# Two ordinary weight tiles after each Strassen tile, and SwiGLU outputs of that stage kept in fp32 until it ends

## The chip, the core and the metric

The kernel runs on one core of a Trainium2 chip. The metric is the device time in microseconds of one execution, taken as the median of the runs. A separate execution is taken with the hardware profiler, and all rows of a trace come from that one. Five engines work side by side, each with a queue of its own: TensorE (PE in the profile, with PEld for its weight loads), VectorE (DVE), ScalarE (ACT), GpSimd (POOL) and SyncE (SP, which issues nearly all DMAs here).

## What is computed

A decoder trunk of two layers on 256 tokens of width 2048, all in float32. The first layer is a recurrent block (RG-LRU) and a SwiGLU feed-forward, the second a sliding-window attention and a SwiGLU feed-forward. The change touches the feed-forward alone, which runs once in each layer:

```python
D_MODEL = 2048; SEQ = 256; D_FF = 5632
def swiglu_ffn(x, g, w_in, w_out):      # w_in: 2048 x 11264, w_out: 5632 x 2048
    h = rms_norm(x, g)
    gate, up = jnp.split(h @ w_in, 2, axis=-1)
    return x + (jax.nn.silu(gate) * up) @ w_out
```

## The kernel before

**Tiles and precision.** Every weight matrix is read once from HBM, as tiles of 128 x 1024 floats (512 KB): 256 rows of the matrix by 512 columns, that is two row blocks of 128 and four column blocks of 128. A float32 product is made from fp32r parts: a number v is split into `hi`, its rounded copy, and `lo = v - hi`, and the product is `hi*hi + hi*lo + lo*hi`, three matmuls of 128 x 256. So each weight tile costs ACT one copy (`hi<-raw`, line 295) and DVE one subtraction (`lo<-raw,hi`, line 298), and then PE 2 x 4 x 3 = 24 matmuls (`products`, line 361). Activations are kept in the same two parts, in one slot of 128 x 512 that holds `hi` and `lo` of 128 features for 256 tokens. Slots (`s` in the profile) come from a first-in first-out list of 58.

**The stream.** All tiles stand in one list, `jobs`, and `stream` walks through it. At tile i it emits the DMA of tile i+4 (`load`), the split of tile i+3 (`split`) and the matmuls of tile i. There are four buffers each of `raw`, `hi` and `lo`, so the split of a tile needs the `hi` buffer of the tile four before it, and a DMA needs the split of the tile four before. Work that is not tied to a tile (epilogues, norms, the attention) is written as generators; `run_bg` steps them twice per tile as long as two running estimates, `self.dve` and `self.act`, stay under a budget. A generator that yields n sleeps n half tiles.

**Ordinary and Strassen tiles.** The 11264 columns of `ffn_in` make 22 groups of 512 columns, 8 tiles each (the 2048 rows). A group holds gate, up, gate, up for two blocks of 128 hidden features. Groups 4 to 21 are *ordinary* (`group`). Groups 0 to 3 (`NS = 4`) are *Strassen* groups: a tile is taken as a 2 x 2 block product and made with 7 block products instead of 8, so 21 matmuls instead of 24 (`strassen`, line 460). For this the tile needs sums of its blocks: `sums` puts three subtractions on POOL (lines 277 to 279, `s<-raw`), and `split` then has three pairs to split instead of one (line 287 on ACT, line 288 on DVE: one 128 x 768 piece `lo<-raw,hi` and two 128 x 512 pieces `s<-s,s`). It also needs sums of the activation blocks, made once for each feed-forward by `form` (lines 488 to 491 on POOL, then a split).

**The order of tiles.** `ffn` writes it by hand: 4 ordinary tiles (`AHEAD`), then Strassen and ordinary tiles in turn, 32 of each, then the remaining ordinary tiles. This stretch, from the first to the last Strassen tile, is called the Strassen stage below; there is one in each feed-forward. A Strassen group holds 4 PSUM banks of the 8 for all its tiles. The ordinary groups beside it are `paired`: their four results share two banks. Unpaired groups take four banks and make some products as one matmul of 128 x 512 instead of two of 128 x 256 (the `"h"` parts in `products`).

**Epilogues.** When a Strassen group ends, `fast` takes its 4 banks to two slots U and V (DVE and ACT), applies SiLU, multiplies gate and up with `stt` (line 134), and four PE transposes (lines 369 and 372) bring the result to features by tokens; then two splits make `hid`, the parts that `ffn_out` will need. When an ordinary group ends, `done` pulls four results, applies SiLU, multiplies (`tt`, line 130) and splits twice. `hid` is first read by `project`, which runs after all of `ffn_in`.

Of the kernel before, what the change touches and what calls it, by code (L numbers as in the profile page):

```python
# [12 lines left out]
F32 = mybir.dt.float32  # L13
F32R = mybir.dt.float32r
AF = mybir.ActivationFunctionType
ALU = mybir.AluOpType
# [3 lines left out]
T = 256  # L20
DFF = 5632
ND = D // P
# [27 lines left out]
class Trunk:  # L50
# [17 lines left out]

    NS = 4
    AHEAD = 4  # L70
    SPACE = 14

    def __init__(self, ctx, tc, dram):
# [355 lines left out]
                    done([(p, two, st["bank"][b] if last_of else None) for p, two, b, last_of in st["ps"]])  # L429
            jobs.append((src(c), mm))  # L430

    def strassen(self, src, xs, forms, done, last):

        st = {}
        jobs = []
        for c in range(ND // 2):
            part = {}

            def mm(hi, lo, c=c, part=part):
                if c == 0:  # L440
                    st["ps"] = [self.bank() for _ in range(4)]
                    st["begun"] = set()
                ps = st["ps"]
                x2 = [self.need(xs[2 * c + kt]) for kt in range(2)]
                fh, fl = self.need(forms[c])
                A = lambda kt, b: tuple(x2[kt][:, q + b * P:q + b * P + P] for q in (0, T))
                S = lambda n: tuple(q[:, n * P:n * P + P] for q in (fh, fl))
                B = lambda n: tuple(q[:, n * T:n * T + T] for q in (hi, lo))
                s = part["set"]
                t1, t3, t2, t4 = (tuple(s[n + q][:, h * T:h * T + T] for q in (0, 1)) for n in (2, 4) for h in range(2))  # L450
                todo = [(0, 0, A(0, 0), B(1)), (1, 1, A(1, 0), B(3)), (1, 0, S(1), t2), (2, 0, S(0), t1),
                        (2, 1, S(2), t3), (3, 0, S(3), B(2)), (3, 1, A(1, 1), t4)]
                if self.other is not None:
                    self.runs = self.RUNS
                    self.other = None
                for n, (b, h, w, m) in enumerate(todo):
                    if n == 4:
                        self.half_tick()
                    for i, j in ((0, 0), (0, 1), (1, 0)):
                        self.nc.tensor.matmul(ps[b][:, h * T:h * T + T], w[i], m[j], start=b not in st["begun"],  # L460
                                              stop=c == ND // 2 - 1 and i == 1, skip_group_check=True)
                        st["begun"].add(b)
                        self.since += 1
                if last and c == ND // 2 - 1:
                    for q in self.sets:
                        for t in q:
                            self.free(t)
                    self.sets = None
                if last:
                    for q in (fh, fl):  # L470
                        self.free(q)
                if c == ND // 2 - 1:
                    done(ps)
            jobs.append((src(c), mm, part))
        return jobs

    def form(self, c, col, out):

        while len(self.slots) < self.SPACE:
            yield 1  # L480
# [156 lines left out]
    def ffn(self, l, xs, forms, r, gains, rn, out=None):  # L637
        hid = [Val() for _ in range(NH)]
        w = self.d[f"ffn_in{l}"]
        one = self.con[:, K_ID:K_ID + P]  # L640
        turns, ordinary = [], []
        for g in range(self.NS):
            def fast(ps, g=g):
                c1, U, V = self.t(), self.slot(F32), self.slot(F32)
                two = lambda q: q.rearrange("p (b t) -> p b t", b=2)
                twice = lambda q: q.unsqueeze(1).broadcast_to([P, 2, T])
                self.a(c1, ps[0][:, 0:T])
                self.tt(two(U[:, :]), two(ps[1][:, :]), twice(c1[:, :]), ALU.add)
                self.tt(two(V[:, :]), two(ps[2][:, :]), twice(U[:, 0:T]), ALU.add)
                self.tt(U[:, 0:T], ps[2][:, 0:T], V[:, T:2 * T], ALU.add)  # L650
                self.tt(V, ps[3], V, ALU.add)
                for b in ps:
                    self.free_bank(b)

                def task():
                    while not self.rv[r].ready:
                        yield 1
                    rs = [self.rstd[r][:, T + b:T + b + 1] for b in range(2)]
                    for q, s in ((U, 0), (V, 1)):
                        self.a(q[:, T:2 * T], q[:, T:2 * T], AF.Silu, scale=rs[s])  # L660
                    yield
                    for q, k, s in ((V, U, 0), (U, V, 1)):
                        self.stt(q[:, 0:T], q[:, 0:T], rs[s], k[:, T:2 * T], ALU.mult, ALU.mult)
                    yield 4
                    while not self.room():
                        yield 1
                    p = self.mbank()
                    for h in range(2):
                        for b, q in enumerate((V, U)):
                            self.pe_other(p[:, h * T + b * P:h * T + b * P + P], q[:, h * P:h * P + P], one,  # L670
                                          f=self.nc.tensor.transpose)
                    yield 1
                    self.free(U)
                    self.free(V)
                    for h in range(2):
                        while not self.slots:
                            yield 1
                        s = self.slot()
                        self.split_act(s, p[:, h * T:h * T + T])
                        hid[2 * g + h].ap = s  # L680
                        hid[2 * g + h].ready = True
                        yield
                    self.free_mbank(p)
                self.spawn(task())
            turns += self.strassen(lambda c, g=g: w[g, c], xs, forms, fast, g == self.NS - 1)
        for g in range(self.NS, NH // 2):
            def done(ps, g=g):
                rs = self.rstd[r][:, 0:T]
                early = not self.rv[r].ready
                v = [self.pull(p, r=None if early else rs) for p in ps]  # L690

                def task():
                    while not self.rv[r].ready:
                        yield 1
                    for h in range(2):
                        ga, up = v[2 * h], v[2 * h + 1]
                        if early:
                            self.tt(ga, ga, rs, ALU.mult)
                            self.tt(up, up, rs, ALU.mult)
                        self.a(ga, ga, AF.Silu)  # L700
                        yield
                        self.tt(ga, ga, up, ALU.mult)
                        while not self.slots:
                            yield 1
                        s = self.slot()
                        self.split_act(s, ga)
                        self.free_half(ga)
                        self.free_half(up)
                        hid[2 * g + h].ap = s
                        hid[2 * g + h].ready = True  # L710
                        yield
                self.spawn(task())
            self.group(lambda c, g=g: w[g, c], ND, xs, done, g == NH // 2 - 1, self.SYNC,
                       paired=2 * (g <= 2 * self.NS), jobs=ordinary)
        n = len(turns)
        self.jobs += ordinary[:self.AHEAD]
        for q in zip(turns, ordinary[self.AHEAD:]):
            self.jobs += q
        self.jobs += ordinary[self.AHEAD + n:]
        self.project(self.d[f"ffn_out{l}"], NH, hid, gains, rn, out)  # L720


# [610 lines left out]
```

## Time and profile before

| | us |
|---|---|
| median of 3 runs (range) | 2023.13 (2022.03 to 2024.72) |
| the profiled execution, its own time | 2023.72 |
| span of that execution, first to last instruction | 2021.9 |
| PE busy | 1985.0 (98%) |
| DVE busy | 1412.9 (70%) |
| ACT busy | 1122.3 (56%) |
| POOL busy | 376.7 (19%) |

A row of instruction groups reads: line, engine, operation, output<-input, shapes, count | busy us, mean ns of one | idle time of the engine before them and what ended it. A row of waits reads: engine, output and line that waited <- what it waited for: us in total, times, longest. A row of the timeline reads: start us, us, engine, line, operation, count. A row of windows gives for a stretch the busy time of PE, PEld, DVE, ACT and POOL (each with its count), the clock granted to PE, and the DMA share. A matmul of 128 x 256 is shown as some 276 ns long, but the next one starts after 113 to 118 ns; so a busy PE may still be late by up to 160 ns per matmul without a gap, and the starts are what to read. A few per cent of the matmul records are missing.

### The profile page before, as it was taken

The page shows a single profiled execution, that of the slowest core. Times are in us where ns is not written, and L with a number is a line of the kernel's source. Part 1 is how long each engine was busy: PE and PEld are TensorE (multiplying, and loading weights), DVE is VectorE, ACT ScalarE, POOL GpSimd, SP SyncE. Part 2 cuts the span into 40 slices and gives each one's busy share as a digit, 9 for nine tenths or more (in the row PEclk, how much of TensorE's full clock was granted, in tenths as well). Part 3 has the DMA queues.
Part 4 walks back from the last instruction along what each step waited for, and adds up shares of the span by engine and source line. Part 5 has one row for each costly group of instructions (what it writes and reads, how often), then busy time and mean ns, then how long its engine had stood idle before and what let it go on. Part 6 is the DMA issues. An engine that isn't in the chain of part 4 may idle for free.

```text
span 2021.9 us, 41009 instructions
## 1 busy us (share of the span) xinstructions
PE 1985.0 (98%) x16699; PEld 1943.6 (96%) x16699; DVE 1412.9 (70%) x2089; ACT 1122.3 (56%) x1754; POOL 376.7 (19%) x356
## 2 busy tenths in 40 slices
PE   9999998999999999999999999989999999999999
PEld 9999998999999999999999889889999999999999
DVE  8988979999655655545667767889866556554553
ACT  6799766555444444434556776555555445444342
POOL 0000136774000000000002453576700000000000
PEclk9999999999999999999999999999999999999999
DMA  8555654555555555555555435455555655556663
GB/s 279 189 182 186 209 173 161 188 180 193 194 198 191 196 192 195 193 194 198 190 190 164 139 123 175 160 173 182 176 192 192 196 195 190 197 197 201 207 209 125
DMA packets 106204, 377.15 MB, mean 187 GB/s; under 512 B 11936, under 2 KB 14368, under 8 KB 106016
## 3 DMA queue, kind: packets, MB, share of 16 engines
q1 hardware_dynamic: 105408, 373.88, 56.0%
q8 instruction: 130, 2.13, 0.4%
q10 hardware_dynamic: 608, 0.66, 0.1%
q14 instruction: 58, 0.48, 0.1%
HBM read 371.88 MB, written 2.10 MB: 185 GB/s over the span
## 4 chain that ended last, share of the span: by engine, by line
PE 83%; DVE 7%; issue 3%; ACT 3%; POOL 2%; DMA 1%; ACTq 0%; DVEq 0%; POOLq 0%; SPq 0%
PE b L361 75%; PE b L460 4%; DVE lo L298 2%; DVE s L288 2%; PE b L372 1%; DVE s L130 1%; ACT hi L295 1%; ACT s L121 1%; DMA raw<-in_ffn_in 1%; DVE lo L288 1%; PE b L826 1%; POOL s L277 1%; PE b L369 1%; POOL s L489 1%; PE b L1012 1%
## 5 line engine op out<-in xcount | busy, mean ns | idle before, releaser
L361 PE MATMUL b<-s,hi 128*128 128x256 f32 (+1 forms) x9474 | 1309.1, 284 | 6.1 <-ACT hi L295 4.9
L361 PEld LDWEIGHTS b<-s,hi 128*128 128x128 f32 x9474 | 1207.5, 189 | 29.0 <-ACT hi L295 5.3
L298 DVE TENSOR_TENSOR lo<-raw,hi 128x1024 fp32r<-128x1024 f32 (+1 forms) x643 | 795.7, 1240 | 501.8 <-ACT hi L295 497.8
L295 ACT ACTIVATE hi<-raw 128x1024 fp32r<-128x1024 f32 (+1 forms) x643 | 675.8, 1054 | 623.4 <-PE b L361 562.1
L361 PE MATMUL b<-s,lo 128*128 128x256 f32 x4992 | 753.1, 277 | 0.0
L361 PEld LDWEIGHTS b<-s,lo 128*128 128x128 f32 x4992 | 655.1, 189 | 0.6
L277 POOL TENSOR_TENSOR s<-raw 128x512 f32<-128x512 f32 x64 | 121.4, 1896 | 115.0 <-DMA raw<-in_ffn_in 98.1
L288 DVE TENSOR_TENSOR s<-s,s 128x512 fp32r<-128x512 f32 x128 | 125.8, 985 | 17.5 <-ACT s L287 17.5
L1102 POOL TENSOR_TENSOR s<-s 128x128 f32<-128x128 f32 x32 | 14.7, 461 | 635.3 <-ACT s L121 630.7
L287 ACT ACTIVATE s<-s 128x512 fp32r<-128x512 f32 x128 | 79.7, 624 | 87.0 <-POOL s L277 48.1
L460 PE MATMUL b<-s,s 128*128 128x256 f32 x768 | 115.4, 283 | 4.4 <-DVE s L288 4.2
L460 PEld LDWEIGHTS b<-s,s 128*128 128x128 f32 x768 | 100.9, 189 | 6.3 <-DVE s L288 6.2
L460 PE MATMUL b<-hi,s 128*128 128x256 f32 x384 | 89.4, 282 | 1.1 <-DVE s L130 0.9
L288 DVE TENSOR_TENSOR lo<-raw,hi 128x768 fp32r<-128x768 f32 x64 | 80.4, 1256 | 0.4
L279 POOL TENSOR_TENSOR s<-raw,s 128x256 f32<-128x256 f32 x64 | 72.5, 1132 | 5.0
L489 POOL TENSOR_TENSOR s<-s 128x128 f32<-128x128 f32 x16 | 16.3, 1017 | 303.4 <-ACT s L121 303.4
L121 ACT ACTIVATE s<-s 128x256 f32<-128x256 f32 (+3 forms) x132 | 51.9, 439 | 37.4 <-POOL s L491 26.4
L460 PEld LDWEIGHTS b<-hi,s 128*128 128x128 f32 x384 | 68.4, 190 | 1.9 <-DVE s L130 1.9
L278 POOL TENSOR_TENSOR s<-raw,s 128x256 f32<-128x256 f32 x64 | 66.5, 1040 | 5.0
L460 PE MATMUL b<-lo,s 128*128 128x256 f32 x192 | 54.6, 284 | 7.6 <-DVE lo L288 7.6
L121 ACT ACTIVATE s<-x,par 128x256 fp32r<-128x256 f32 (+1 forms) x112 | 52.7, 497 | 16.4 <-DVE x L130 11.2
L130 DVE TENSOR_TENSOR s<-s,s 128x256 fp32r<-128x256 f32 (+3 forms) x100 | 46.1, 489 | 20.9 <-ACT s L121 20.9
(120 smaller groups left out, 1188.6 us busy)
## 6 DMA issues: line engine op xcount, KB each, us to landing
raw<-in_ffn_in SPq DMA_DIRECT2D x352, 512.0 KB, 3.4
raw<-in_ffn_out SPq DMA_DIRECT2D x176, 512.0 KB, 3.3
raw<-in_lru_in SPq DMA_DIRECT2D x62, 512.0 KB, 3.6
raw<-in_lru_out SPq DMA_DIRECT2D x32, 512.0 KB, 4.2
raw<-in_w_q SPq DMA_DIRECT2D x32, 512.0 KB, 3.4
raw<-in_w_o SPq DMA_DIRECT2D x32, 512.0 KB, 3.3
raw<-in_gate SPq DMA_DIRECT2D x8, 512.0 KB, 3.7
raw<-in_kv SPq DMA_DIRECT2D x8, 512.0 KB, 4.3
```

The lines of the kernel that those rows point to most:

```text
L121: self.nc.scalar.activation(out, in_, func, **kw)
L130: self.nc.vector.tensor_tensor(out, a, b, op)
L277: tt(two(s[0][:, :]), b[:, 0:3:2, :], b[:, 1::-1, :], ALU.subtract)
L278: tt(s[1][:, 0:T], raw[:, 2 * T:3 * T], s[0][:, 0:T], ALU.subtract)
L279: tt(s[1][:, T:2 * T], raw[:, 3 * T:4 * T], s[1][:, 0:T], ALU.subtract)
L287: self.nc.scalar.activation(a, z, AF.Copy)
L288: self.nc.vector.tensor_tensor(b, z, a.bitcast(F32), ALU.subtract)
L295: high = self.ins(self.nc.scalar.activation(hi[:, q], raw[:, q], AF.Copy))
L298: self.nc.vector.tensor_tensor(lo[:, q], raw[:, q], hi[:, q].bitcast(F32), ALU.subtract)
L361: self.nc.tensor.matmul(*args, **kw)
L460: self.nc.tensor.matmul(ps[b][:, h * T:h * T + T], w[i], m[j], start=b not in st["begun"], stop=c == ND // 2 - 1 and i == 1, skip_group_ch ...
L489: tt(s[2], a11, a21, ALU.subtract)
```

## The change

After each Strassen tile come two ordinary tiles instead of one (`OWN = 2`), so that the 32 Strassen tiles of a feed-forward stand among 64 ordinary ones, and ordinary groups up to 12, not 8, are paired. Groups that end while Strassen tiles are still to come no longer split their SwiGLU outputs at once: the two blocks of a group are kept as one fp32 slot, and a new generator `later` splits them when the last Strassen tile has been emitted (`left[0]` is 0). A Strassen group copies its transposed result from PSUM with one ACT copy of 128 x 512 and splits from there.

```diff
-    def strassen(self, src, xs, forms, done, last):
+    def strassen(self, src, xs, forms, done, last, left):
 ...
+                left[0] -= 1
 ...
+        left = [self.NS * ND // 2]
+
+        def later(g, s):
+            while left[0]:
+                yield 1
+            for h in range(2):
+                while len(self.slots) < 2:
+                    yield 1
+                q = self.slot()
+                self.split_act(q, s[:, h * T:h * T + T])
+                hid[2 * g + h].ap = q
+                hid[2 * g + h].ready = True
+                yield
+            self.free(s)
 ...                                                  (fast, after the transposes into p)
-                    for h in range(2):
-                        while not self.slots:
-                            yield 1
-                        s = self.slot()
-                        self.split_act(s, p[:, h * T:h * T + T])
-                        hid[2 * g + h].ap = s
-                        hid[2 * g + h].ready = True
-                        yield
+                    s = self.slot(F32)
+                    self.a(s, p)
                     self.free_mbank(p)
+                    yield
+                    yield from later(g, s)
 ...                                                  (done of an ordinary group)
+                        if both is not None or h == 0 and left[0]:
+                            if h == 0:
+                                both = self.slot(F32)
+                            self.tt(both[:, h * T:h * T + T], ga, up, ALU.mult)
+                            self.free_half(ga)
+                            self.free_half(up)
+                            yield
+                            continue
 ...
+                    if both is not None:
+                        yield from later(g, both)
 ...
-                       paired=2 * (g <= 2 * self.NS), jobs=ordinary)
+                       paired=2 * (g <= (self.OWN + 1) * self.NS), jobs=ordinary)
 ...
-        for q in zip(turns, ordinary[self.AHEAD:]):
-            self.jobs += q
-        self.jobs += ordinary[self.AHEAD + n:]
+        for i, q in enumerate(turns):
+            k = self.AHEAD + self.OWN * i
+            self.jobs += [q] + ordinary[k:k + self.OWN]
+        self.jobs += ordinary[self.AHEAD + self.OWN * n:]
```

Counted over the whole built program, 63 matmuls of 128 x 512 become 126 of 128 x 256, and nothing else changes on PE but the order. SP issues the same 734 DMAs and POOL the same 361 instructions. DVE has 16 instructions fewer and ACT 8 fewer (results of unpaired groups come in two halves that are added; four groups in each feed-forward no longer need this). Twelve groups in each feed-forward, 4 Strassen and 8 ordinary, have their 24 splits put off. The line numbers of the changed kernel are one or more higher than those of the kernel before.

**DVE at the end of the first Strassen group.** Here `lo<-raw,hi` and `s<-s,s` are splits of coming tiles, `s<-b,...` take the four banks to U and V, and SCALAR_TENSOR_TENSOR are the two products that the transposes need. Before:

```order
L130 TENSOR_TENSOR s_4349<-b_85,t_92 128x512
L130 TENSOR_TENSOR s_4350<-b_86,s_4349 128x512
L288 TENSOR_TENSOR s_3724<-s_3721,s_3723 128x512
L130 TENSOR_TENSOR s_4349<-b_86,s_4350 128x256
L288 TENSOR_TENSOR lo_81<-raw_73,hi_77 128x768
L130 TENSOR_TENSOR s_4350<-b_87,s_4350 128x512
L288 TENSOR_TENSOR s_3726<-s_3722,s_3725 128x512
L298 TENSOR_TENSOR lo_82<-raw_74,hi_78 128x1024
L134 SCALAR_TENSOR_TENSOR s_4350<-s_4350,rstd_104,s_4349 128x256
L134 SCALAR_TENSOR_TENSOR s_4349<-s_4349,rstd_104,s_4350 128x256
```

Four splits of weight tiles stand among the four bank reads and ahead of the products. The same place in the changed kernel:

```order
L131 TENSOR_TENSOR s_4539<-b_85,t_92 128x512
L131 TENSOR_TENSOR s_4540<-b_86,s_4539 128x512
L131 TENSOR_TENSOR s_4539<-b_86,s_4540 128x256
L131 TENSOR_TENSOR s_4540<-b_87,s_4540 128x512
L299 TENSOR_TENSOR lo_80<-raw_72,hi_76 128x1024
L135 SCALAR_TENSOR_TENSOR s_4540<-s_4540,rstd_104,s_4539 128x256
L135 SCALAR_TENSOR_TENSOR s_4539<-s_4539,rstd_104,s_4540 128x256
```

Now one split stands ahead of the products. On PE, the four transposes of each of the first three groups stood 36 matmuls behind the last one of their group in the first feed-forward and 45 in the second; now they stand 69 and 60 behind it.

**POOL at the opening of the first Strassen stage.** L277 to L279 (L278 to L280 in the changed kernel) are the sums of one Strassen tile, the other rows are the last two `form`s. Before:

```order
L489 TENSOR_TENSOR s_3887<-s_3886 128x128
L488 TENSOR_TENSOR s_3887<-s_3886 128x128
L490 TENSOR_TENSOR s_3887<-s_3887,s_3886 128x128
L489 TENSOR_TENSOR s_3895<-s_3894 128x128
L491 TENSOR_TENSOR s_3887<-s_3886,s_3887 128x128
L277 TENSOR_TENSOR s_3715<-raw_71 128x512
L278 TENSOR_TENSOR s_3716<-raw_71,s_3715 128x256
L279 TENSOR_TENSOR s_3716<-raw_71,s_3716 128x256
L488 TENSOR_TENSOR s_3895<-s_3894 128x128
L490 TENSOR_TENSOR s_3895<-s_3895,s_3894 128x128
L491 TENSOR_TENSOR s_3895<-s_3894,s_3895 128x128
```

The third Strassen tile's sums stood inside the last form. The same place in the changed kernel:

```order
L491 TENSOR_TENSOR s_3853<-s_3852 128x128
L278 TENSOR_TENSOR s_3721<-raw_74 128x512
L490 TENSOR_TENSOR s_3853<-s_3852 128x128
L279 TENSOR_TENSOR s_3722<-raw_74,s_3721 128x256
L492 TENSOR_TENSOR s_3853<-s_3853,s_3852 128x128
L280 TENSOR_TENSOR s_3722<-raw_74,s_3722 128x256
L493 TENSOR_TENSOR s_3853<-s_3852,s_3853 128x128
L490 TENSOR_TENSOR s_3861<-s_3860 128x128
L491 TENSOR_TENSOR s_3861<-s_3860 128x128
L492 TENSOR_TENSOR s_3861<-s_3861,s_3860 128x128
L493 TENSOR_TENSOR s_3861<-s_3860,s_3861 128x128
```

The second Strassen tile's sums now stand among the steps of the form before the last, and the last form follows without a break.

More of the change, by code (lines that the diff above doesn't have):

```diff
@@ L70 @@
     AHEAD = 4
+    OWN = 2
     SPACE = 14
@@ L674, in task @@
                     self.free(V)
-                    for h in range(2):
-                        while not self.slots:
-                            yield 1
-                        s = self.slot()
-                        self.split_act(s, p[:, h * T:h * T + T])
-                        hid[2 * g + h].ap = s
-                        hid[2 * g + h].ready = True
-                        yield
+                    s = self.slot(F32)
+                    self.a(s, p)
                     self.free_mbank(p)
+                    yield
+                    yield from later(g, s)
                 self.spawn(task())
-            turns += self.strassen(lambda c, g=g: w[g, c], xs, forms, fast, g == self.NS - 1)
+            turns += self.strassen(lambda c, g=g: w[g, c], xs, forms, fast, g == self.NS - 1, left)
         for g in range(self.NS, NH // 2):
@@ L694, in task @@
                         yield 1
+                    both = None
                     for h in range(2):
```

## The prediction

> **What bounds the kernel now.** I read the page first, then the windows of the two Strassen stages beside a stretch of ordinary tiles, then PE's waits in each stage, and last the timeline for the length of single tiles.
>
> ```profile
> span 2021.9 us, 41009 instructions
> PE 1985.0 (98%) x16699; PEld 1943.6 (96%) x16699; DVE 1412.9 (70%) x2089; ACT 1122.3 (56%) x1754; POOL 376.7 (19%) x356
> PE   9999998999999999999999999989999999999999
> ```
>
> PE bounds the kernel nearly everywhere, so the time falls only where PE waits or runs slowly. The windows go from the first to the last Strassen matmul of each feed-forward; the third one holds ordinary tiles alone.
>
> ```profile
> 304.10:493.80 189.70, 175.18 (x1435) 171.01 (x1434) 176.78 (x195) 106.49 (x167) 130.29 (x98) 0.99 0.53 177
> 1287.00:1481.10 194.10, 178.91 (x1436) 176.05 (x1435) 175.73 (x197) 108.29 (x167) 131.70 (x98) 0.96 0.54 176
> 550.00:800.00 250.00, 250.00 (x2101) 245.69 (x2100) 151.72 (x212) 121.25 (x164) 0.00 (x0) 1.00 0.59 194
> ```
>
> In the stages PE is idle for 14.5 and 15.2 us, DVE is busy for 93% and 91%, POOL for 69% and 68%, and the granted clock dips. With ordinary tiles PE is never idle and DVE is at 61%. What PE waits for in the first stage, and then in the second:
>
> ```profile
> PE b L460 <- DVE lo L288: 5.5, 5, 1.6
> PE b L361 <- ACT hi L295: 4.7, 1, 4.7
> PE b L369 <- DVE s L134: 2.0, 3, 0.7
> PE b L460 <- DVE s L288: 1.4, 4, 0.8
> ```
> ```profile
> PE b L369 <- DVE s L134: 9.5, 3, 3.8
> PE b L460 <- DVE s L288: 2.9, 4, 1.9
> PE b L460 <- DVE lo L288: 2.0, 2, 1.8
> ```
>
> All but one are DVE being late: with the splits of a Strassen tile (L288) or with the products ahead of the transposes (L134). These idle times leave out what the modelled matmul ends cover, so I go by starts of tiles. An ordinary tile ahead of the stage, a Strassen and an ordinary tile inside it, and the ordinary tiles behind it, in the timeline of PE:
>
> ```profile
> 296.02 1.98 PE L361 MATMUL b<-s,hi 128*128 128x256 f32 x16
> ...
> 298.74 1.98 PE L361 MATMUL b<-s,hi 128*128 128x256 f32 x16
> ...
> 398.60 0.28 PE L460 MATMUL b<-hi,s 128*128 128x256 f32 x1
> ...
> 401.06 2.05 PE L361 MATMUL b<-s,hi 128*128 128x256 f32 x16
> ...
> 403.89 0.28 PE L460 MATMUL b<-hi,s 128*128 128x256 f32 x1
> ...
> 494.07 2.05 PE L361 MATMUL b<-s,hi 128*128 128x256 f32 x16
> ...
> 496.90 2.05 PE L361 MATMUL b<-s,hi 128*128 128x256 f32 x16
> ...
> 510.06 1.09 PE L361 MATMUL b<-s,hi 128*128 128x512 f32 x5
> ```
> ```profile
> L295 ACT ACTIVATE hi<-raw 128x1024 fp32r<-128x1024 f32 x92 | 97.7, 1062 | 128.1 <-PE b L361 110.1 <-issue 18.0
> ```
>
> An ordinary tile takes 2.72 us outside the stage (296.02 to 298.74; 92 tiles in the window of 250 us give 2.72 too). Inside it takes 2.83 us even where nothing waits (401.06 to 403.89), and so still behind it (494.07 to 496.90), until unpaired groups with 128x512 matmuls begin at 510. A Strassen tile without a wait takes 2.46 us. So without any wait a stage would be 32 x 2.46 + 31 x 2.83 + about 2 for 18 small matmuls (transposes, norm) = 168.4 us. It takes 189.7 and 194.1: **21.3 and 25.7 us are lost**, 47 in all.
>
> **The change part by part.**
>
> *More ordinary tiles in the stage.* 31 tiles for each feed-forward move from behind the stage, where they cost 2.72 us, between its first and last Strassen tile, where they cost 2.83. A stage without waits is then 32 x 2.46 + 62 x 2.83 + 2 = 256.2 us; today's stage with the 31 tiles behind it is 189.7 + 84.3 = 274.0 and 194.1 + 84.3 = 278.4. The most that the change can bring is so 17.8 + 22.2 = 40 us. It holds the price of the slower pace, 2 x 31 x 0.11 = 6.8 us, already. That price is bounded by 0 (the paired tiles at 296 ran at 2.72 with no Strassen tile among them) and 6.8; I take 6.8, since the paired tiles at 494 to 500 kept the pace of the stage with no Strassen tile left.
>
> *What is left of the waits* depends on DVE's share. The rows of DVE that grow, go or wait, first stage, then the split of an ordinary tile and of an output outside it:
>
> ```profile
> L298 DVE TENSOR_TENSOR lo<-raw,hi 128x1024 fp32r<-128x1024 f32 x33 | 46.9, 1424 | 0.3
> L130 DVE TENSOR_TENSOR s<-h,s 128x256 fp32r<-128x256 f32 x8 | 7.2, 897 | 0.0
> L130 DVE TENSOR_TENSOR s<-b,s 128x256 fp32r<-128x256 f32 x6 | 2.5, 417 | 0.0
> L288 DVE TENSOR_TENSOR s<-s,s 128x512 fp32r<-128x512 f32 x63 | 63.9, 1016 | 6.4 <-ACT s L287 6.4
> ```
> ```profile
> L298 DVE TENSOR_TENSOR lo<-raw,hi 128x1024 fp32r<-128x1024 f32 x92 | 112.6, 1224 | 98.8 <-ACT hi L295 98.6
> L130 DVE TENSOR_TENSOR s<-h,s 128x256 fp32r<-128x256 f32 x24 | 9.0, 419 | 0.0
> L121 ACT ACTIVATE s<-h 128x256 fp32r<-128x256 f32 x24 | 8.5, 402 | 0.0
> ```
>
> DVE's 176.8 us in the first stage gain 31 splits of 1.42 = 44, and four ordinary epilogues of six instructions of about 0.42 = 10; the output splits, 7.2 for the ordinary groups and 2.5 for the Strassen ones, leave. That makes 221 us in 256, 86% instead of 93%. POOL's 130 us spread to 51%. A split may be about two tiles late before PE notices (it is emitted three tiles ahead), and the slack of a Strassen tile with its two neighbours is 8.12 - 221 / 32 = 1.2 us, where today the work of a pair, 176.8 / 32 = 5.5, stands against 5.29 of PE. So DVE turns from late to early, and PE is the bound. What I leave of the waits, each between 0 and what it is today:
>
> - Splits of Strassen tiles (L288): 6.9 and 4.9 us today. Left: 1 in each stage.
> - Transposes (L369 behind L134): 2.0 and 9.5 us. The order shown in the section on the change has one split instead of four ahead of the products, and 69 and 60 matmuls instead of 36 and 45 to cover them, 8.1 and 7.1 us at 2.83 / 24 = 0.118. Today's worst case shows the queue of DVE:
>
> ```profile
> 1344.34 0.68 DVE L130 TENSOR_TENSOR s<-b,s 128x512 f32<-128x512 f32 x1
> ...
> 1345.54 0.87 DVE L134 SCALAR_TENSOR_TENSOR s<-s,rstd,s 128x256 f32<-128x256 f32 x2
> ...
> 1346.07 0.47 PE L369 MATMUL b<-con,s 128*128 128x128 f32 x1 [3.83 <-DVE s L134]
> ```
> ```profile
> 1346.00:1352.00 6.00, 5.93 (x29) 5.72 (x30) 3.95 (x7) 2.85 (x6) 4.14 (x3) 0.54 0.62 208
> ```
>
>   There 45 matmuls (5.3 us) were 3.83 us too few, so 9.1 would have been needed with DVE four splits behind; in the first stage 36 matmuls (4.2) were 0.7 too few, so 4.9. Both are the ends; three splits fewer (each 0.7 to 1.2) bring the worst to about 6, under 7.1. Left: 0.5 and 1.5. With the wait goes the half clock behind it: 6 us at 0.54 cost 2.8.
> - The opening: in the first stage 4.7 us (PE waits for a `hi` of ACT, which is blocked behind a form that POOL has not finished, the row below), in the second the L288 waits of 1.9 and 1.8. The last form no longer has sums in its middle, but the norm (its reciprocal and products) and the forms still fall on DVE and POOL there. Left: 2.5 and 2.5.
>
> ```profile
> 315.15 0.63 ACT L121 ACTIVATE s<-s 128x512 fp32r<-128x512 f32 x1 [4.20 <-POOL s L491]
> ```
>
> - The put-off splits: 24 x 0.42 us on DVE and 24 x 0.40 on ACT, 10 us of each behind each stage, where DVE is busy for 61% and ACT for 48%, so some 25 us of slack lie in each 65 us of tiles; `project` reads `hid` hundreds of us later. They cost between 0 and 10 a feed-forward; I take 0.5. The whole 128x512 ACT copies and the fp32 slots lie beside matmuls: ACT has 44% of the stage free, and PE's ordinary tiles do not read them.
>
> The sum left is 2 + 2 + 5 + 1 = 10 us, so 40 - 10 = 30 us gained. The profiled execution took 2023.72 us, of which 1.8 lie outside the span; 2023.7 - 30 = 1993.7. The median is 0.6 below that execution, so **1993 us**.
>
> **The rivals.**
>
> *DVE and POOL exclude each other, and half of the loss stays.* DVE's splits and POOL's sums both read slots, and both get longer together. Their shortest durations beside their medians in the first stage:
>
> ```profile
> L288 DVE TENSOR_TENSOR s<-s,s x63: 676/691/1792, 303.9 to 489.4; 128x512 fp32r<-128x512 f32 x63
> L288 DVE TENSOR_TENSOR lo<-raw,hi x31: 943/1104/2052, 307.9 to 488.5; 128x768 fp32r<-128x768 f32 x31
> L298 DVE TENSOR_TENSOR lo<-raw,hi x33: 1209/1217/2315, 304.9 to 491.1; 128x1024 fp32r<-128x1024 f32 x33
> L277 POOL TENSOR_TENSOR s<-raw x30: 1267/1740/4153, 310.2 to 482.0; 128x512 f32<-128x512 f32 x30
> L278 POOL TENSOR_TENSOR s<-raw,s x30: 737/1068/1806, 311.8 to 483.5; 128x256 f32<-128x256 f32 x30
> L279 POOL TENSOR_TENSOR s<-raw,s x30: 723/1097/1603, 312.9 to 484.7; 128x256 f32<-128x256 f32 x30
> ```
>
> The shortest times add up to 42.6 + 29.2 + 39.9 on DVE and 81.8 on POOL, 193.5 us, and about 11 us of epilogue products come on top: 204 in a stage of 189.7. So they overlap a little, and nearly exclude each other. Taken as one resource they would need 204 + 31 x 1.21 = 242 of the new 256 us, 95%, which leaves bursts (openings, group ends) hardly any room. If half of today's 47 us stayed, the time would be 2023.7 - 40 + 23.5 = 2007. Against it stands that 204 is already 8% more than the stage took; scaled so, 242 is 225, 88%. The Trainium skill, "SBUF — State Buffer", section "Who interferes with whom", says that a DVE instruction with two SBUF inputs and a GpSimd instruction that reads SBUF block each other for the whole instruction; by that rule the sum would be this rival's 2007, by DVE's own busy share it is 1993. The trace agrees with it only in part, by the 204 in 189.7. Chance 0.16.
>
> *Slower: the loss belongs to each Strassen tile, not to DVE's share.* If a Strassen tile's own chain (DMA, sums on POOL, copies on ACT, splits on DVE) is what is late, each of the 64 tiles keeps its 47 / 64 = 0.73 us, and the slower pace of 6.8 us is all that is added: 2030. It decides from 40 us left, 0.63 a tile. For it: PE's waits are at L460 and L369, Strassen work. Against it: the chain has one ordinary tile more of room, and DVE itself waits only 6.4 us on ACT in the first stage. Chance 0.06.
>
> *The put-off splits are exposed.* If all 10 us of them fell on PE in each feed-forward, 1993.7 + 20 = 2013. DVE's 39% of free time there speaks against it. Chance 0.03.
>
> *The pace of 2.72 comes back inside the stage.* 124 ordinary tiles x 0.11 = 13.6 us more: 1980. Nothing but the tiles at 296 speaks for it. Chance 0.03.
>
> **How the numbers follow.** The forecast itself, 5 to 22 us left of the waits, has 0.72: 1988 to 2005. A measurement of this kernel can tell about 0.2%, 4 us, from no change. Faster by more: the forecast, most of the first rival and the last two, 0.90; within: the far end of the first rival, 0.04; slower: 0.06. The low end, 1984, is the sum with no wait left (40 us), the high end, 2011, takes in most of the first rival.
>
> **What would show it.** After the change, the stage (first to last Strassen matmul) should take 256 to 266 us, with DVE at 84 to 89%; PE's waits on L134 should be under 2 us in the second stage, with at most two dips of the clock; ordinary tiles inside should still start 2.83 us apart; the put-off splits should make PE wait for nothing. I am wrong if DVE stays above 92% in the longer stage, or if PE's waits on splits of Strassen tiles stay at 5 us and more.

## The result, and the profile after

The changed kernel is slower: 2100.24 us median of 3 runs (2099.38 to 2103.38) against 2023.13, a ratio of 1.0384 with a 95% interval of 1.0361 to 1.0408. The forecast was 1993 us, with a chance of 0.06 for slower. The page of the changed kernel (line numbers are one or two higher from here on, and up to seven more in the runs below that add lines):

```profile
span 2101.6 us, 41038 instructions
PE 2014.5 (96%) x16762; PEld 1967.6 (94%) x16762; DVE 1344.7 (64%) x2073; ACT 1119.1 (53%) x1746; POOL 329.9 (16%) x356
```

The two Strassen stages, from the first to the last Strassen matmul, in windows (PE, PEld, DVE, ACT and POOL busy, then the clock and the DMA share):

```profile
304.20:619.90 315.70, 276.01 (x2180) 269.09 (x2179) 190.38 (x251) 143.87 (x212) 110.58 (x100) 0.96 0.47 156
1329.60:1645.00 315.40, 275.11 (x2180) 267.76 (x2180) 189.47 (x251) 144.80 (x213) 108.20 (x101) 0.96 0.47 157
```

Each stage takes some 315.5 us where 256.2 had been worked out for no wait at all: 59.5 and 59.2 us are lost, 118.7 in all. Less the 40 us that the longer stage was to bring, that is 78.7, and the span grew by 79.7. What differs from the picture before is that no engine is full: PE is busy for 87% of the first stage, DVE for 60% (93% before), POOL for 35%, ACT for 46%. All of them wait. The longest waits of the first stage (PE's is its longest), and then the longest of the queue of the DMAs (SPq) there:

```profile
POOL s L278 <- DMA raw<-in_ffn_in: 170.3, 27, 8.6
ACT s L288 <- POOL s L278: 107.3, 31, 5.4
DVE s L289 <- ACT s L288: 105.8, 51, 4.4
ACT s L288 <- POOL s L280: 40.1, 29, 2.4
PE b L362 <- ACT hi L296: 17.7, 18, 1.6
```
```profile
SPq L253 <- DVE lo L299: 147.3, 48, 7.3
```

Read in this order they close a ring: POOL's sums wait for the DMA, ACT's copies of the sums wait for POOL, DVE's splits wait for ACT, and the DMA waits for `lo` of DVE (L299, the split of an *ordinary* tile). PE comes last and waits for a `hi` (L296), the ordinary tile's too. One turn of the ring in the timeline (start, duration):

```profile
406.55 1.29 POOL L278 TENSOR_TENSOR s<-raw 128x512 f32<-128x512 f32 x1 [6.34 <-DMA raw<-in_ffn_in]
...
407.87 0.63 ACT L288 ACTIVATE s<-s 128x512 fp32r<-128x512 f32 x1 [4.37 <-POOL s L278]
407.92 0.74 POOL L279 TENSOR_TENSOR s<-raw,s 128x256 f32<-128x256 f32 x1
...
408.73 1.10 POOL L280 TENSOR_TENSOR s<-raw,s 128x256 f32<-128x256 f32 x1
409.86 0.63 ACT L288 ACTIVATE s<-s 128x512 fp32r<-128x512 f32 x1 [1.36 <-POOL s L280]
410.40 1.04 ACT L296 ACTIVATE hi<-raw 128x1024 fp32r<-128x1024 f32 x1
...
411.47 1.23 DVE L299 TENSOR_TENSOR lo<-raw,hi 128x1024 fp32r<-128x1024 f32 x1 [0.26 <-ACT hi L296]
...
416.11 1.98 POOL L278 TENSOR_TENSOR s<-raw 128x512 f32<-128x512 f32 x1 [6.28 <-DMA raw<-in_ffn_in]
...
426.41 1.30 POOL L278 TENSOR_TENSOR s<-raw 128x512 f32<-128x512 f32 x1 [6.32 <-DMA raw<-in_ffn_in]
```

The sums of a Strassen tile start when its DMA has landed (406.55), the second copy on ACT ends at 410.49, then come `hi` and `lo` of the ordinary tile ahead of it (to 412.70), and only then can the next Strassen tile's DMA be issued. Its sums start 3.4 us later (416.11). The next turn ends at 426.41. A turn takes 9.6 to 10.3 us, and PE has work for 2.46 + 2 x 2.83 = 8.1. It is so through the whole stage: the 31 first sums from 303.7 to 608.2 start 10.15 us apart on average.

That the ordinary tile's `hi` stands behind the Strassen tile's copies is a matter of ACT's queue. The layer that builds the program moves instructions of one engine past each other, so the queue is not the order in which `split` writes them, as its built order shows. ACT's queue in the kernel before, and in the changed one (copies and `hi` alone; a few other instructions stand between them):

```
L287 ACTIVATE s_3719<-s_3716 128x512
L295 ACTIVATE hi_76<-raw_72 128x1024
L287 ACTIVATE s_3723<-s_3721 128x512
L287 ACTIVATE hi_77<-raw_73 128x768
L287 ACTIVATE s_3725<-s_3722 128x512
L295 ACTIVATE hi_78<-raw_74 128x1024
```
```
L296 ACTIVATE hi_77<-raw_73 128x1024
L288 ACTIVATE s_3717<-s_3715 128x512
L288 ACTIVATE s_3719<-s_3716 128x512
L296 ACTIVATE hi_78<-raw_74 128x1024
L288 ACTIVATE hi_75<-raw_71 128x768
```

Before, the copies of a Strassen tile (`s_3723`, `s_3725` beside `hi_77` 128x768) stand behind `hi` of the ordinary tile ahead of it (`hi_76`). Now both copies (`s_3717`, `s_3719`, of the tile in `raw_71`) stand ahead of `hi_78`, of the ordinary tile in `raw_74`, the tile before. And `raw_74` is the buffer that the next Strassen tile, three tiles on, gets: with four buffers, tile i+4 takes that of tile i. Before, Strassen tiles came every second tile, used `raw_71` and `raw_73` only, and each followed a Strassen tile in its buffer.

### The profile page after: what moved, and what is told of

It is laid out like the page before. It is cut to its first block, busy times and chain, and to the rows that moved or that the text cites. A ratio compares the mean times of both kernels' runs of the same rounds, so it can differ in the third digit from the quotient of the medians.

```text
span 2101.6 us, 41038 instructions
## 1 busy us (share of the span) xinstructions
PE 2014.5 (96%) x16762; PEld 1967.6 (94%) x16762; DVE 1344.7 (64%) x2073; ACT 1119.1 (53%) x1746; POOL 329.9 (16%) x356
## 4 chain that ended last, share of the span: by engine, by line
PE 66%; POOL 9%; DMA 8%; DVE 7%; ACT 6%; issue 4%; POOLq 0%; ACTq 0%; DVEq 0%
PE b L362 60%; DMA raw<-in_ffn_in 8%; DVE lo L299 4%; POOL s L278 3%; ACT hi L296 3%; POOL s L280 2%; POOL s L279 2%; ACT s L122 2%; PE b L461 1%; PE b L373 1%; PE b L851 1%; PE b L370 1%; DVE s L131 1%; PE b L1037 1%; POOL s L491 0%
## 5 line engine op out<-in xcount | busy, mean ns | idle before, releaser
L362 PE MATMUL b<-s,hi 128*128 128x256 f32 (+1 forms) x9535 | 1323.2, 285 | 32.6 <-ACT hi L296 31.2
L362 PEld LDWEIGHTS b<-s,hi 128*128 128x128 f32 x9535 | 1219.7, 190 | 59.6 <-ACT hi L296 38.6
L299 DVE TENSOR_TENSOR lo<-raw,hi 128x1024 fp32r<-128x1024 f32 (+1 forms) x643 | 787.8, 1228 | 440.2 <-ACT hi L296 437.8
L296 ACT ACTIVATE hi<-raw 128x1024 fp32r<-128x1024 f32 (+1 forms) x643 | 674.1, 1052 | 516.3 <-PE b L362 471.5
L289 DVE TENSOR_TENSOR s<-s,s 128x512 fp32r<-128x512 f32 x128 | 90.3, 707 | 211.9 <-ACT s L288 211.8
L278 POOL TENSOR_TENSOR s<-raw 128x512 f32<-128x512 f32 x64 | 94.7, 1479 | 407.5 <-DMA raw<-in_ffn_in 379.2
L122 ACT ACTIVATE s<-s 128x256 fp32r<-128x256 f32 (+3 forms) x180 | 69.9, 429 | 33.8 <-POOL s L493 22.1
L131 DVE TENSOR_TENSOR s<-s,s 128x256 fp32r<-128x256 f32 (+3 forms) x148 | 64.3, 460 | 20.9 <-ACT s L122 20.8
L280 POOL TENSOR_TENSOR s<-raw,s 128x256 f32<-128x256 f32 x64 | 66.9, 1046 | 4.9
L289 DVE TENSOR_TENSOR lo<-raw,hi 128x768 fp32r<-128x768 f32 x64 | 62.2, 972 | 0.3 <-ACT hi L288 0.2
L122 ACT ACTIVATE s<-x,par 128x256 fp32r<-128x256 f32 (+1 forms) x112 | 52.8, 498 | 16.8 <-DVE x L131 11.2
L288 ACT ACTIVATE hi<-raw 128x768 fp32r<-128x768 f32 x64 | 53.1, 829 | 0.0
```

The source lines that it names most:

```text
L122: self.nc.scalar.activation(out, in_, func, **kw)
L131: self.nc.vector.tensor_tensor(out, a, b, op)
L278: tt(two(s[0][:, :]), b[:, 0:3:2, :], b[:, 1::-1, :], ALU.subtract)
L280: tt(s[1][:, T:2 * T], raw[:, 3 * T:4 * T], s[1][:, 0:T], ALU.subtract)
L288: self.nc.scalar.activation(a, z, AF.Copy)
L289: self.nc.vector.tensor_tensor(b, z, a.bitcast(F32), ALU.subtract)
```

## The experiments

The theory is this ring. Its rivals were that the put-off splits and fp32 slots cost the time, that four raw buffers are too few whatever ACT's order, and that DVE and POOL exclude each other. All runs below stand beside runs of the kernel before on the same chip (medians 2022.1 to 2023.8 there).

**1. ACT's order put right.** One edge in `split` keeps the copies of the sums behind the last ordinary `hi`:

```diff
-            high = self.ins(self.nc.scalar.activation(hi[:, q], raw[:, q], AF.Copy))
+            high = self.high = self.ins(self.nc.scalar.activation(hi[:, q], raw[:, q], AF.Copy))
 ...                                   (Strassen tile, for the two sums)
-                self.nc.scalar.activation(a, z, AF.Copy)
+                    with self.tc.issue_after(self.high):
+                        self.nc.scalar.activation(a, z, AF.Copy)
```

> The changed kernel, with one edge more: on ACT the two copies of a Strassen tile's sums may not be issued ahead of the hi copy of the ordinary tile before it. Loop theory: in the changed kernel the next Strassen tile's DMA (3.4 us) waits for lo of an ordinary tile, whose hi (1.04) and lo (1.23) stand on ACT behind the copy (0.63) that waits for the sums on POOL (3.1 to 3.3) of the present Strassen tile, which wait for its DMA: 9.6 to 10.3 us a round, against 8.1 us of PE. With the edge the round is open, PE bounds the stage (256 to 266 us instead of 315.7) and the time is 1985 to 2005 us. Rival, ring too short: four raw buffers are too few for a Strassen tile in every one of them, whatever ACT's order; the time stays within 2090 to 2105. Rival, put-off splits and fp32 slots: nothing changes, 2095 to 2105.

Measured: 1992.95 us, ratio to the kernel before 0.985 (0.9833 to 0.9866). The stages in windows:

```profile
302.40:561.20 258.80, 256.92 (x2180) 256.27 (x2179) 225.93 (x254) 145.86 (x212) 140.39 (x100) 1.00 0.59 191
1270.70:1531.10 260.40, 257.18 (x2180) 256.14 (x2179) 218.80 (x254) 145.99 (x212) 131.63 (x100) 1.00 0.58 189
```

One ordering edge on ACT was added, and 107 us are gone: the stages take 258.8 and 260.4 us, PE is idle for 1.9 and 3.2, the clock stays at 1.00, DVE is at 87% and 84%. PE's waits in the first stage are down to two of 0.9 us (transposes, then a Strassen split):

```profile
PE b L376 <- DVE s L136: 0.9, 1, 0.9
PE b L467 <- DVE lo L295: 0.9, 1, 0.9
```

The put-off splits and the four buffers are still in this kernel, so neither costs the time by itself; the order on ACT closed the ring. POOL's built order at the opening of the stage moved along with the edge (and in the same way in run 5), which alone can't account for it: the turns of the changed kernel are long through the whole stage, not at its opening.

**2. The put-off splits alone.** `OWN = 1`, so tiles stand as before:

```diff
-    OWN = 2
+    OWN = 1
```

> The changed kernel with OWN = 1: the order of tiles of the kernel before, with the outputs kept in fp32 and split at the end of the stage. Loop theory: the put-off splits have no part in it, 2013 to 2028 us (0 to 10 us faster than before, since the splits leave the stage in which DVE is at 93%). Rival, put-off splits and fp32 slots: they carry most of the 77 us, so 2060 to 2100.

Measured: 2022.23 us, ratio 0.9995 (0.9985 to 1.0004). Keeping the outputs in fp32 and splitting them later costs nothing that can be measured, and brings nothing either.

**3. The second sum made twice, in the changed kernel.**

```diff
+        tt(s[1][:, 0:T], raw[:, 2 * T:3 * T], s[0][:, 0:T], ALU.subtract)
         tt(s[1][:, 0:T], raw[:, 2 * T:3 * T], s[0][:, 0:T], ALU.subtract)
```

> The changed kernel with the second sum on POOL (0.74 us alone) made twice for each of the 64 Strassen tiles. Loop theory: it lies on the round, so 64 x 0.74 = 47 us more: 2140 to 2155 us. Rival, DVE and POOL exclude each other: DVE is at 55 to 60% and POOL at 38% of the stage, so the doubled sum finds room: less than 10 us more, 2100 to 2110. Rival, the ring is too short at the DMA alone: also less than 10.

Measured: 2153.21 us, 53 us more than the changed kernel. The stages:

```profile
302.70:643.40 340.70, 285.64 (x2180) 277.95 (x2179) 193.62 (x254) 144.94 (x214) 133.36 (x132) 0.92 0.44 145
1352.70:1692.90 340.20, 278.76 (x2180) 270.82 (x2179) 193.23 (x253) 145.53 (x214) 134.26 (x132) 0.95 0.44 146
```

25 us more in each stage, 0.78 for each of 32 tiles, where the instruction takes 0.74 alone. POOL is busy for 39% of the stage, and the added instruction is paid in full all the same: it lies on the ring.

**4. The same doubled sum with ACT's order put right.**

> The kernel with the edge on ACT, and the second sum on POOL made twice as well. Loop theory: the round is open, so the same 0.74 us a tile is hidden: within 8 us of the kernel with the edge. Rival, ring too short: the sums stay on the path, 47 us more than the kernel with the edge.

Measured: 2024.5 us, 31.5 more than in 1. This was a miss: the time was to be hidden. The stages, and a turn of a longer ring that the timeline shows to be left:

```profile
305.20:581.30 276.10, 264.08 (x2180) 260.99 (x2179) 232.92 (x251) 142.74 (x210) 167.40 (x132) 0.98 0.55 177
1290.70:1568.90 278.20, 264.23 (x2180) 261.27 (x2179) 234.84 (x251) 142.04 (x210) 165.50 (x131) 0.98 0.54 176
```

```profile
403.99 1.63 POOL L279 TENSOR_TENSOR s<-raw 128x512 f32<-128x512 f32 x1 [3.12 <-DMA raw<-in_ffn_in]
...
409.06 1.07 POOL L282 TENSOR_TENSOR s<-raw,s 128x256 f32<-128x256 f32 x1
410.15 0.63 ACT L295 ACTIVATE s<-s 128x512 fp32r<-128x512 f32 x1 [3.87 <-POOL s L282]
...
411.43 1.99 ACT L303 ACTIVATE hi<-raw 128x1024 fp32r<-128x1024 f32 x2
...
412.51 3.46 DVE L306 TENSOR_TENSOR lo<-raw,hi 128x1024 fp32r<-128x1024 f32 x2
...
420.27 1.80 POOL L279 TENSOR_TENSOR s<-raw 128x512 f32<-128x512 f32 x1 [1.75 <-DMA raw<-in_ffn_in]
```

Four sums (to 410.13), the copy, `hi` and `lo` of the two ordinary tiles behind (to 415.97), and the DMA of the Strassen tile *after the next* into the second one's buffer (420.27): 16.28 us for two Strassen tiles, for which PE has 16.24. This turn is one of the short ones, and alone would cost nothing: from the first to the 31st tile of the stage (302.8 to 569.7) the sums start 8.90 us apart on average, 17.8 for two tiles, where run 1 has 8.20 (309.5 to 547.3, 30 tiles). Where DVE and POOL run at once, both get longer besides (the two `lo` take 3.46 us instead of 2 x 1.22). So the ring and the lengthening come together here. The alternative is that the lengthening alone is the cause; run 6 opens the ring and leaves the lengthening.

**5. Five raw buffers, ACT's order left as the change has it.**

```diff
-    LD = 4
+    LD = 5
-    SPACE = 14
+    SPACE = 12
-        self.slots = deque(range(58))
+        self.slots = deque(range(56))
-        self.raw = [const.tile([P, 1024], F32, name=f"raw{i}") for i in range(4)]
+        self.raw = [const.tile([P, 1024], F32, name=f"raw{i}") for i in range(5)]
```

> The changed kernel, without the edge, with five raw buffers instead of four (DMAs five tiles ahead; 56 slots instead of 58, and 12 instead of 14 free ones asked for by form). Loop theory: the next Strassen tile's DMA now waits for lo of the ordinary tile one earlier, whose hi stands on ACT behind the first of the two copies only, which needs the first sum alone: 3.4 (DMA) + 1.3 (sum) + 0.63 + 1.04 + 1.23 = 7.6 us a round, under PE's 8.1, so PE bounds again: 1988 to 2012 us. Rival: the casts ahead of hi in ACT's queue cost their wait in each Strassen tile whatever the ring: 2085 to 2105.

Measured: 1999.97 us, ratio 0.9888 (0.9873 to 0.9902); the stages take 262.6 and 267.5 us. A second cure for the same ring, at another link, as expected; the first copy still stands ahead of an ordinary `hi`, and some 7 us more than in 1 are left. So the copies at the head of ACT's queue did nearly all their harm through the Strassen DMA that waited behind them.

**6. Five buffers, ACT's order and the doubled sum.**

> The edge, five raw buffers and the doubled second sum. It is to tell why the doubled sum cost 31 us in the kernel with the edge. Second round: with the edge a longer round remains over two Strassen tiles (DMA to landing, four sums, copy, hi of the Strassen and of two ordinary tiles, their lo, next but one Strassen DMA), 16.3 us in that kernel's trace at 404 to 420 against 16.3 of PE; five buffers take one hi and one lo off it, about 2.5 us, so the doubled sum is hidden: 1985 to 2003 us. Rival, DVE and POOL exclude each other: the ring changes nothing, 2015 to 2030.

Measured: 1991.96 us (two runs). Against 1987.89 without the doubled sum (8, below, on another chip) that is 4.1 us, not 31.5. The two Strassen stages of this run in windows, and the same windows of the run without the doubled sum (8, a little shorter in its stages):

```profile
304.10:562.90 258.80, 256.63 (x2180) 256.17 (x2179) 236.61 (x258) 147.03 (x214) 152.68 (x127) 1.00 0.59 194
1272.30:1533.30 261.00, 257.02 (x2180) 256.16 (x2179) 235.87 (x257) 146.43 (x212) 154.09 (x127) 1.00 0.60 192
```
```profile
304.10:562.90 258.80, 258.18 (x2193) 257.72 (x2192) 221.06 (x260) 149.40 (x214) 112.14 (x96) 1.00 0.60 196
1272.30:1533.30 261.00, 258.49 (x2195) 257.83 (x2194) 221.80 (x261) 150.63 (x216) 112.72 (x94) 1.00 0.59 194
```

The extra sums would add some 32 x 0.74 = 24 us to POOL alone; POOL has 41 more and DVE 14 to 15 more, so the two do lengthen each other here. The stage takes 258.8 and 261.0 us all the same, with PE idle for 2.2 and 4.0. So the lengthening by itself does not cost 4 its 31.5 us; it does so where a DMA waits at the end of the ring.

**7. ACT's order put right at `OWN = 1`.**

> The edge on ACT at OWN = 1, the order of tiles before. Loop theory: there the hi copies of the ordinary tiles stand ahead of the sums' copies already, DVE and POOL are what is late, and the edge brings nothing: 2017 to 2028 us. Rival: the edge itself removes a round that the kernel before has as well, and most of the gain of the kernel with the edge is its own: under 2008.

Measured: 2020.6 us, ratio 0.9991 (0.9981 to 1.0). In the order of tiles before, the edge finds nothing to open. So the gain of 1 over the kernel before is not the edge's own: it takes the new order of tiles.

**8. Five buffers and ACT's order.**

> The edge and five raw buffers, without the doubled sum. The stage of the kernel with the edge alone has 2.6 us and 4.2 us left above 256.2; if both rounds are open these go, and nothing else moves: 1986 to 1992 us. Rival, DVE and POOL exclude each other and set what is left: 1992 to 1996, as with the edge alone.

Measured: 1987.89 us, ratio 0.9827 (0.9811 to 0.9843), the fastest of all. The stages take 257.3 and 259.3 us, with 256.2 worked out.

**9. Five Strassen groups, with ACT's order.**

```diff
-    NS = 4
+    NS = 5
```

> The kernel with the edge and five Strassen groups instead of four in each feed-forward (40 Strassen and 80 ordinary tiles in the stage). Loop theory with PE the bound: 16 tiles at 2.46 instead of 2.72 or 2.83 us, and 32 more ordinary tiles at 2.83 instead of 2.72: 5.9 - 3.5, about 2.5 us faster than the kernel with the edge, 1986 to 1994 us. Rival, DVE at 87% has no room for more: the stage's waits grow, 1995 to 2010.

Measured: 1989.88 us, ratio 0.9838 (0.9821 to 0.9854), 3 us less than 1, as worked out from the lengths of tiles; the two intervals overlap, so that the step itself is not shown.

## Why the prediction was wrong

The step that failed is the part "What is left of the waits depends on DVE's share", the term of 10 us: it measured 118.7. The list there took each wait of before and left of it a value "between 0 and what it is today", so a new wait had no place in it. What filled that place was a round through four queues, which no share of busy time shows: in the longer stage DVE fell to 60%, lower than the 86% that were forecast, and the stage got longer by the very waiting that made room on every engine. The built orders of PE, DVE and POOL stand in the text ahead of the result, ACT's does not: ACT was counted as 44% free. It was in ACT's queue that two copies had moved ahead of an ordinary tile's `hi`.

The rival "slower" named the chain (DMA, sums on POOL, copies on ACT, splits on DVE) but priced it at today's 0.73 us a Strassen tile and said that an ordinary tile more gives it room. Run 3 shows the true price: a duration on the chain counts in full, 0.78 us for an instruction of 0.74, and a turn costs 9.6 to 10.3 us against 8.1, some 1.85 us a tile. The extra tile gave no room, because that tile itself stood in the chain.

Point by point, the rest:

- The stage without waits, 256.2 us, and the slower pace inside it: right. The changed kernel's ordinary tiles start 2.82 us apart where nothing waits:

```profile
409.95 2.05 PE L362 MATMUL b<-s,hi 128*128 128x256 f32 x16
...
412.77 2.05 PE L362 MATMUL b<-s,hi 128*128 128x256 f32 x16
```

  Run 8 comes within 1.1 and 3.1 us of 256.2. It gains 34.8 us on the kernel before, and with these 4.2 us that is 39.0 of the 40 that the change could bring at most. With ACT's order put right (run 1) 2.6 and 4.2 us of waits are left, 6.8 where the forecast had some 10, and DVE's share is 87% and 84% where it had 86%. That the time of run 1, 1992.95 us, is the forecast to a tenth is chance: its four executions lie between 1989.5 and 1994.1. It was a forecast for another queue of ACT.
- Transposes: wrong with the ring, right without it. In the changed kernel they cost PE more than before, 13.3 and 15.4 us, though DVE had more free time. The product on DVE waits for a SiLU on ACT (L122), the engine whose queue is held up by the copies (the first stage):

```profile
PE b L373 <- DVE s L135: 8.4, 3, 4.0
DVE s L135 <- ACT s L122: 8.0, 3, 3.8
PE b L370 <- DVE s L135: 4.9, 3, 2.4
```

  With the order put right (run 1) 0.9 us is left in each stage; 0.5 and 1.5 were forecast.
- The put-off splits: right that they are hidden (run 2). The rival that they are exposed falls.
- DVE and POOL exclude each other: as the bound of the stage it falls. The stage of run 1 comes within 2.6 us of PE's 256.2 at 87% of DVE and 54% of POOL. The Trainium skill, "SBUF — State Buffer", "Who interferes with whom", says that a DVE instruction with two SBUF inputs contends with a GpSimd instruction that reads SBUF, and calls contention an exclusive lock; that the loser waits for the whole instruction it says of DVE's two-port modes. The runs agree that the two delay each other (the `lo` of 3.46 us in run 4, the sum on POOL below). They don't agree that one stands still for as long as the other works: in the first stage of run 6 the shortest durations alone, times their counts, are 147 us for the weight splits on DVE, 21 for its other instructions with two inputs in SBUF and 105 for the sums on POOL, 273 together in a stage of 258.8.

```profile
L278 POOL TENSOR_TENSOR s<-raw x31: 1277/1296/2379, 303.7 to 608.2; 128x512 f32<-128x512 f32 x31
```

  In the changed kernel, where DVE and POOL are busy at once for 45 of 315.7 us of the first stage by the trace, the median of the first sum is 1296 ns. Before the change, where they are so for 129 of 189.7, it was 1740, with nearly the same shortest one.
- The signs that were to show it wrong, DVE above 92% or 5 us and more of PE's waits on Strassen splits, would have caught the rivals that were thought of. In the first stage neither came, and in the second only the latter, barely (5.6 us behind `lo` of Strassen tiles); the forecast was wrong by far more than that tells.

How much of the 118.7 us is half clock and how much is the ring alone stays open: the granted clock was 0.96 in these stages, but a PE that waits for the ring would have lost part of that time anyhow.

## What to carry to other kernels

Where tiles of two kinds share a ring of buffers, follow the reuse of one buffer through every queue that it passes, and add up the turn: DMA, each engine's instruction, and whatever stands ahead of it in that engine's queue. If the turn is longer than the bound engine's work for as many tiles, it sets the time, and all shares of busy time fall. When the period of the kinds changes, look at the built order of every engine, the idle ones too; two copies for each Strassen tile, moved ahead of one `hi` on an engine at 46%, cost 107 us here. One ordering edge brought them back, one more buffer 100 of them.

## What the runs showed of the hardware

An instruction on the ring was paid one for one (0.74 us alone, 0.78 us a tile in run 3). ACT's copies waited for POOL for up to 5.4 us at a time, and ACT ran nothing from behind them meanwhile: the `hi` that started at 410.40 is of a tile whose DMA had landed at 400.79, by the trace. The pace of 2.83 us an ordinary tile holds inside a stage even where nothing waits, in the kernels before and after (2.82 in the rows above), and is 2.72 again only well behind it; what sets it was not tried.
